# Adaptive-norm modulation in 1024-column pieces summed by transposes, and half of an output projection on both streams at once

## The chip, the cores and the metric

The program runs on one core of one Trainium2 chip. The metric is device time in microseconds (us) of one execution. Before the change it is 2055.41 us (median of 3 runs, 2054.89 to 2059.09).

## What is computed

Two transformer blocks follow one another on 256 tokens of width 1024; the part that matters here is layer 0 of the first. It has two streams, `x` (tile `X` in the kernel, stream 0) and `ctx` (tile `C`, stream 1), each 256 tokens.

```python
for i in range(DEPTH):                       # 2 layers
    mod   = silu(c)     @ w_ada[i] + b_ada[i]   # 6*1024 values, six pieces of 1024
    mod_c = silu(c_ctx) @ w_ada[i] + b_ada[i]
    sh1, sc1, g1, sh2, sc2, g2 = split(mod, 6)
    h = modulate(rms_norm(x), sh1, sc1); hc = the same of ctx with mod_c
    # layer 0: short convolution; layer 1: neighbourhood attention
    b_gate, c_gate, u = split(h @ conv_w_in, 3)
    y = (b_gate * conv3(c_gate * u)) @ conv_w_out
    x = x + g1 * y
    x = x + g2 * swiglu(modulate(rms_norm(x), sh2, sc2), ffn_w_in[i], ffn_w_out[i])
    # and ctx alike with mod_c, in layer 0
```

After it come attention, and a second network of feed-forward blocks and mixers, which the change leaves alone.

## The kernel before

Activations stand transposed, features on partitions and tokens in columns. All weights come through one stream (`WeightStream`): a list of units of 512 KB in the order of use, loaded by SyncE's DMA queue into 5 raw buffers (`raw_bufs`). A unit of a projection is split by ScalarE (`whi`, L106) and VectorE (`wlo`, L107) into a high and a low part, in 4 buffers, and each product is three matmuls (`mm3`, L243 to L245). A unit marked raw is not split. With both streams side by side a matmul has 512 columns, with one stream 256.

The modulation is a matrix times two vectors. The first four pieces of 512 outputs are made by matmuls at the start (`ada_direct`, `ada_fast`); the change touches `ada_slow`, which makes the other 20, (0, 4) to (0, 11) and (1, 0) to (1, 11). For each 128 rows of `w_ada`, VectorE multiplies the rows by one vector's values, one per partition, and adds to an accumulator of 128 x 512 (L476 for the first, L478 for the others), for one vector or for two. The accumulator is split into `ada_hi` and `ada_lo`; TensorE sums it over partitions by matmuls with a selecting matrix `pick` (L489, L490), ScalarE copies the row out, and four small transposes (L441) turn it into columns, to which L444 adds the bias. `ADA_AT` says at which step each piece's four units stand in the stream and are used: after each group of the convolution, after groups of `conv_w_out` for stream 0, and between the groups of the feed-forward.

`conv_block` runs four groups of the convolution's input products (six units a group, 512 columns), then `conv_w_out`: all four groups for stream 0, then all four for stream 1 (256 columns; 16 units). After a stream's groups, its sum of squares goes through matmuls (`rstd_cols`, L361), VectorE makes the inverse square root with ten tiny operations (`newton`, L265 to L269, between L364 and L374), a matmul spreads it over partitions (L376), and `modulate` (L538, L540, then `xh` and `xl`) writes what the feed-forward reads. The first feed-forward group (`ffn`, `first`) uses its four units for stream 0 and then for stream 1, so that stream 0's 96 matmuls run while stream 1 is still being modulated. Earlier, `modulate(0)` and `modulate(1)` inside `conv_block` do the same for the halves of the convolution's input; the second starts with `modA` (L515).

A scheduler decides the order of instructions on each engine when the program is built; each engine then runs its own list in that order.

Of the kernel before, what the change touches and what calls it, by code (L numbers as in the profile page):

```python
# [7 lines left out]
F32 = mybir.dt.float32  # L8
# [7 lines left out]
P = 128  # L16
D = 1024
# [25 lines left out]
def _pack_layout():  # L43
# [15 lines left out]
NPACK = _pack_layout()  # L59
CCOLS = {  # L60
    "ident": (0, 128), "upper": (128, 256), "tri_st": (256, 384),
    "qk_both": (384, 640), "qk_low": (512, 640), "inv_freq": (640, 656), "pick": (656, 660),
}
NCONST = 660

# [100 lines left out]
class Net:  # L166
# [230 lines left out]
    def ada_start(self):  # L397
        nc = self.nc
        sil = self.sil = self.cp.tile([P, 16], F32, name="sil")
        self.pick = self.cp.tile([P, 4], F32R, name="pick")  # L400
        nc.scalar.copy(self.pick, self.k("pick"))
        self.ada_pending = []
        nc.scalar.activation(sil, self.pk[:, 0:16], AF.Silu)
        self.c4 = self.cp.tile([P, KB, 4], F32R, name="c4")
        for v in range(2):
            s = sil[:, 8 * v : 8 * v + 8]
            self.split(self.c4[:, :, 2 * v], self.c4[:, :, 2 * v + 1], s)
# [55 lines left out]

    def ada_slow(self, layer, j, vecs):

        nc = self.nc
        accs = [self.adap.tile([P, 512], F32, name="ada_acc", tag=f"acc{v}") for v in range(vecs)]
        done = 0
        while done < KB:
            w, _, nk, _ = self.ws.take()  # L470
            for kk in range(nk):
                kb = done + kk
                for v in range(vecs):
                    c = self.sil[:, 8 * v + kb : 8 * v + kb + 1]
                    if kb == 0:
                        nc.vector.tensor_scalar(accs[v], w[:, kk, :], c, None, ALU.mult)  # L476
                    else:
                        nc.vector.scalar_tensor_tensor(accs[v], w[:, kk, :], c, accs[v], ALU.mult, ALU.add)  # L478
            done += nk
        parts = []  # L480
        for v in range(vecs):
            hi = self.adap.tile([P, 512], F32R, name="ada_hi", tag="hi")
            lo = self.adap.tile([P, 512], F32R, name="ada_lo", tag="lo")
            self.split(hi, lo, accs[v])
            parts.append((hi, lo))
        yield
        ps = self.aux_bank()
        for v, (hi, lo) in enumerate(parts):
            nc.tensor.matmul(ps[0:2, :], self.pick[:, 2 * v : 2 * v + 2], hi, start=v == 0, stop=False)  # L489
            nc.tensor.matmul(ps[0:2, :], self.pick[:, 2 * v : 2 * v + 2], lo, start=False, stop=v == vecs - 1)  # L490
        row = self.tmp()
        nc.scalar.copy(row[0:2, :], ps[0:2, :])
        yield
        self.ada_columns(layer, j, row)

    def ada_at(self, *at):
        self.ada_pending = [g for g in self.ada_pending if next(g, WAIT) is None]
        for layer, j in ADA_AT.get(at, []):
            g = self.ada_slow(layer, j, ada_vecs(layer, j))
            next(g)  # L500
            self.ada_pending.append(g)

    def ada_flush(self):
        for g in self.ada_pending:
# [40 lines left out]
    def gated_add(self, layer, piece, kb, v, dst, ps):  # L545
        self.nc.vector.scalar_tensor_tensor(dst[:, kb, :], ps, self.mvec(layer, piece, kb, v), dst[:, kb, :], ALU.mult, ALU.add)

    def block_squares(self, src, kb, accs):

        nc = self.nc  # L550
        sq = self.tmp()[:, :T]
        nc.scalar.activation(sq, src[:, kb, :], AF.Square)
        if not accs:
            return [sq]
        if kb == KB - 1:
            return accs + [sq]
        new = self.rp.tile([P, 512], F32, name="acc1", tag="acc")[:, :T]
        nc.vector.tensor_tensor(new, accs[0], sq, ALU.add)
        return [new]


    def ffn(self, xh, xl, sh, sl, parts, evac, between):
# [4 lines left out]
        for part, (b0, b1) in enumerate(parts):  # L567
            for g in range(b0 // 2, b1 // 2):
                gate = [self.main_bank() for _ in range(2)]
                up = [self.main_bank() for _ in range(2)]  # L570
                if first:
                    units = [self.ws.take() for _ in range(4)]
                    for v in range(2):
                        vs = slice(v * T, (v + 1) * T)
                        for i, dst in enumerate((gate, up)):
                            for h in range(2):
                                self.wstat_unit(units[2 * i + h], [d[:, vs] for d in dst], xh[:, :, vs], xl[:, :, vs], k8, 4 * h)
                else:
                    self.wstat(gate, xh, xl, k8)
                    self.wstat(up, xh, xl, k8)  # L580
                first = False
                for c in range(2):
                    blk = 2 * g + c - b0
                    sg = self.tmp()
                    nc.scalar.activation(sg, gate[c], AF.Silu)
                    s = self.tmp()
                    nc.vector.tensor_tensor(s, up[c], sg, ALU.mult)
                    self.split(sh[:, blk, :], sl[:, blk, :], s)
                between("hid", g)
            kall = list(range(b1 - b0))  # L590
            if part == len(parts) - 1:
                for v in range(2):
# [81 lines left out]
ADA_DIRECT = (0, 2)  # L674


ADA_AT = {
    ("conv", 0): [(0, 4)], ("conv", 1): [(0, 5)], ("conv", 2): [(0, 6)], ("conv", 3): [(0, 7)],
    ("conv_out", 0): [(0, 8)], ("conv_out", 2): [(0, 9)],
    ("hid", 0): [(0, 10)], ("hid", 1): [(0, 11)],  # L680
    ("hid", 2): [(1, 0)], ("hid", 3): [(1, 1)], ("hid", 4): [(1, 2)], ("hid", 5): [(1, 3)],
    ("out", 0): [(1, 4)], ("out", 1): [(1, 5)], ("out", 2): [(1, 6)], ("out", 3): [(1, 7)],
    ("hid", 6): [(1, 8)], ("hid", 7): [(1, 9)], ("hid", 8): [(1, 10)], ("hid", 9): [(1, 11)],
}


def ada_specs(w, *at):
    s = []
    for layer, j in ADA_AT.get(at, []):
        s += ada_units(w[layer], j, True)  # L690
    return s


def ada_vecs(layer, j):
    return 2 if layer == 0 or j < 4 else 1


def stream_specs(a):
# [5 lines left out]
    for k0 in (0, 4):  # L704
        for c0 in (1024, 2048):
            s += cols_units(a["conv_w_in"], c0, 256, k8[k0 : k0 + 4])
        if k0 == 0:
            for i in range(2, 4):
                s += ada_units(w[0], ADA_FIRST[i], ADA_FIRST[i] in ADA_DIRECT)
    for g in range(4):  # L710
        for c0 in (1024, 2048, 0) if g > 0 else (0,):
            s += cols_units(a["conv_w_in"], c0 + g * 256, 256, k8)
        s += ada_specs(w, "conv", g)
    for v in range(2):
        for g in range(4):
            s += cols_units(a["conv_w_out"], g * 256, 256, k8)
            if v == 0:
                s += ada_specs(w, "conv_out", g)
    for part, (b0, b1) in enumerate(FFN0_PARTS):
        for g in range(b0 // 2, b1 // 2):  # L720
            s += cols_units(a["ffn_w_in"][0], g * 256, 256, k8)
            s += cols_units(a["ffn_w_in"][0], HID + g * 256, 256, k8)
            s += ada_specs(w, "hid", g)
        for v in range(1 + (part == len(FFN0_PARTS) - 1)):
            for j in range(4):
                s += cols_units(a["ffn_w_out"][0], j * 256, 256, list(range(b0, b1)))
                if part == 0:
                    s += ada_specs(w, "out", j)
# [30 lines left out]
def conv_block(net):  # L759
# [60 lines left out]
        net.wstat_unit(first[i], pcu[i], xh, xl, k8, 0)  # L820
    modulate(1)
    early.close()
    for i in range(2):
        net.wstat_unit(net.ws.take(), pcu[i], xh, xl, k8, 4)
    with tc.tile_pool(name="hid0", bufs=1) as hp, tc.tile_pool(name="ada", bufs=2) as net.adap:
        sh = hp.tile([P, 12, 512], F32R, name="sh")
        sl = hp.tile([P, 12, 512], F32R, name="sl")
        with tc.tile_pool(name="conv", bufs=1) as zp:
# [4 lines left out]
            for g in range(4):  # L833
                if g == 0:
                    pc, pu = pcu
                else:
                    pc = [net.main_bank() for _ in range(2)]
                    net.wstat(pc, xh, xl, k8)
                    pu = [net.main_bank() for _ in range(2)]
                    net.wstat(pu, xh, xl, k8)  # L840
                pb = [net.main_bank() for _ in range(2)]
                net.wstat(pb, xh, xl, k8)
                for c in range(2):
# [13 lines left out]
                net.ada_at("conv", g)  # L857
            for v in range(2):
                accs = []
                for g in range(4):  # L860
                    ps = [net.main_bank()[:, :T] for _ in range(2)]
                    net.wstat(ps, sh[:, :, vsl[v]], sl[:, :, vsl[v]], k8)
                    for c in range(2):
                        net.gated_add(0, 2, 2 * g + c, v, both[v], ps[c])
                        accs = net.block_squares(both[v], 2 * g + c, accs)
                    if v == 0:
                        net.ada_at("conv_out", g)
                if v == 0:
                    net.ada_flush()
                    for half in range(2):  # L870
                        net.mod_scale(0, 1, half)
                net.modulate(0, 1, v, both[v], net.row_stats(accs), k8, xh[:, :, vsl[v]], xl[:, :, vsl[v]])
        state = {}

        def evac(part, j, c, ps, v):
# [1056 lines left out]
```

## Time and profile before

| | |
|---|---|
| median of 3 runs | 2055.41 us |
| the profiled execution | 2058.65 us, its span 2056.7 us |
| TensorE busy (PE) | 2020.6 us, 98% of the span |
| VectorE busy (DVE) | 1522.3 us, 74% |
| ScalarE busy (ACT) | 1060.0 us, 52% |
| mean granted TensorE clock | 0.997 |

The profile's own time is 3.24 us above the median; sums are made against the profile. PE is matmul time, PEld the weight loads beside it. Ends of matmuls are modelled, so a matmul's own duration (0.39 us for 512 columns) is longer than the distance from one start to the next, and it is the distance that adds up.

### The profile page before, as it was taken

The page shows a single profiled execution, that of the slowest core. Times are in us where ns is not written, and L with a number is a line of the kernel's source. Part 1 is how long each engine was busy: PE and PEld are TensorE (multiplying, and loading weights), DVE is VectorE, ACT ScalarE, POOL GpSimd, SP SyncE. Part 2 cuts the span into 40 slices and gives each one's busy share as a digit, 9 for nine tenths or more (in the row PEclk, how much of TensorE's full clock was granted, in tenths as well). Part 3 has the DMA queues.
Part 4 walks back from the last instruction along what each step waited for, and adds up shares of the span by engine and source line. Part 5 has one row for each costly group of instructions (what it writes and reads, how often), then busy time and mean ns, then how long its engine had stood idle before and what let it go on. Part 6 is the DMA issues. An engine that isn't in the chain of part 4 may idle for free. (4 is left out here: it accounts for less than half of the span.)

```text
span 2056.7 us, 32409 instructions
## 1 busy us (share of the span) xinstructions
PE 2020.6 (98%) x12430; PEld 1775.2 (86%) x12430; DVE 1522.3 (74%) x2796; ACT 1060.0 (52%) x1763; POOL 4.1 (0%) x24
## 2 busy tenths in 40 slices
PE   6999999999999999999999999999999999999999
PEld 3888888888899999888888889998888888989888
DVE  6979998766377778766677767787767776887764
ACT  4534533323355566655455546555545555675552
POOL 0000000000000000000000000000000000000000
PEclk9999999999999999999999999999999999999999
DMA  7746566666254324465566564556556656425654
GB/s 251 230 144 195 175 208 199 215 191 200 88 167 146 98 88 138 144 190 180 183 191 188 181 189 132 154 167 192 184 179 191 185 182 193 136 83 168 186 180 133
DMA packets 327435, 350.93 MB, mean 171 GB/s; under 512 B 12593, under 2 KB 301489, under 8 KB 327281
## 3 DMA queue, kind: packets, MB, share of 16 engines
q1 hardware_dynamic: 327280, 348.88, 54.9%
q8 instruction: 97, 1.59, 0.3%
q14 instruction: 58, 0.47, 0.1%
HBM read 347.78 MB, written 1.05 MB: 170 GB/s over the span
## 5 line engine op out<-in xcount | busy, mean ns | idle before, releaser
L106 ACT CAST whi<-wraw 128x512 fp32r<-128x512 f32 (+1 forms) x803 | 615.2, 789 | 714.2 <-issue 252.3
L107 DVE TENSOR_TENSOR wlo<-wraw,whi 128x512 fp32r<-128x512 f32 (+1 forms) x803 | 708.6, 898 | 341.8 <-ACT whi L106 340.5
L306 PE MATMUL pg<-x,whi 128*128 128x512 f32 x1408 | 387.9, 397 | 0.5 <-DVE x L255 0.3
L306 PEld LDWEIGHTS pg<-x,whi 128*128 128x128 f32 x1408 | 241.0, 188 | 33.9 <-DVE x L255 2.8
L306 PE MATMUL po<-s,whi 128*128 128x512 f32 x880 | 243.1, 394 | 0.0
L308 PEld LDWEIGHTS pg<-x,wlo 128*128 128x128 f32 x1408 | 215.1, 188 | 31.8
L308 PE MATMUL pg<-x,wlo 128*128 128x256 f32 x1408 | 223.3, 280 | 0.0
L243 PE MATMUL pm<-xh,whi 128*128 128x512 f32 (+1 forms) x576 | 217.1, 381 | 3.1 <-ACT xh L251 3.1
L244 PE MATMUL pm<-xl,whi 128*128 128x512 f32 (+1 forms) x576 | 218.3, 380 | 0.0
L245 PE MATMUL pm<-xh,wlo 128*128 128x512 f32 (+1 forms) x576 | 218.0, 379 | 0.0
L478 DVE SCALAR_TENSOR_TENSOR ada_acc<-wraw,sil,ada_acc 128x512 f32<-128x512 f32 x224 | 159.3, 747 | 25.1 <-DMA wraw<-in_w_ada 23.9
L306 PEld LDWEIGHTS po<-s,whi 128*128 128x128 f32 x880 | 148.7, 189 | 18.1
L308 PEld LDWEIGHTS po<-s,wlo 128*128 128x128 f32 x880 | 137.5, 188 | 20.6
L308 PE MATMUL po<-s,wlo 128*128 128x256 f32 x880 | 142.6, 280 | 0.0
L243 PEld LDWEIGHTS pm<-xh,whi 128*128 128x128 f32 x576 | 109.3, 191 | 25.5 <-ACT xh L251 3.8
L245 PEld LDWEIGHTS pm<-xh,wlo 128*128 128x128 f32 x576 | 109.2, 190 | 20.5
L244 PEld LDWEIGHTS pm<-xl,whi 128*128 128x128 f32 x576 | 109.4, 190 | 20.3 <-issue 0.2
L245 PE MATMUL pm<-sh,wlo 128*128 128x256 f32 (+1 forms) x384 | 119.2, 311 | 0.4 <-DVE wlo L107 0.4
L243 PE MATMUL pm<-sh,whi 128*128 128x256 f32 (+1 forms) x384 | 119.2, 311 | 0.0
L244 PE MATMUL pm<-sl,whi 128*128 128x256 f32 (+1 forms) x384 | 118.9, 310 | 0.0
L306 PE MATMUL pg<-xh,whi 128*128 128x512 f32 x352 | 97.8, 399 | 1.9 <-DVE xh L252 1.9
L245 PE MATMUL pm<-whi,xl 128*128 128x256 f32 x352 | 99.6, 283 | 0.0
(435 smaller groups left out, 3456.1 us busy)
## 6 DMA issues: line engine op xcount, KB each, us to landing
wraw<-in_ffn_w_in SPq DMA_DIRECT2D x264, 512.0 KB, 3.8
wraw<-in_ffn_w_out SPq DMA_DIRECT2D x128, 512.0 KB, 3.5
wraw<-in_w_ada SPq DMA_DIRECT2D x96, 512.0 KB, 4.5
wraw<-in_a_w_in SPq DMA_DIRECT2D x28, 512.0 KB, 3.7
wraw<-in_conv_w_in SPq DMA_DIRECT2D x24, 512.0 KB, 4.8
wraw<-in_attn_w_qkv SPq DMA_DIRECT2D x24, 512.0 KB, 4.0
wraw<-in_conv_w_out SPq DMA_DIRECT2D x16, 512.0 KB, 4.3
wraw<-in_ffn_w_out SPq DMA_DIRECT2D x28, 256.0 KB, 2.7
```

The source lines that it names most:

```text
L106: self.nc.scalar.copy(hi[:, cs], raw[:, cs])
L107: self.nc.vector.tensor_tensor(lo[:, cs], raw[:, cs], hi[:, cs].bitcast(F32), ALU.subtract)
L243: mm(ps, ah, bh, start=first, stop=False)
L244: mm(ps, ah, bl, start=False, stop=False)
L245: mm(ps, al, bh, start=False, stop=last)
L306: self.nc.tensor.matmul(pss[c], hi[:, kk, cs], x2[:, done + kk], start=done + kk == 0, stop=False)
L308: self.nc.tensor.matmul(pss[c][:, 0, :], lo[:, kk, cs], x2[:, done + kk, 0, :], start=False, stop=done + kk == nblocks - 1)
L478: nc.vector.scalar_tensor_tensor(accs[v], w[:, kk, :], c, accs[v], ALU.mult, ALU.add)
```

## The change

The 20 pieces of 512 outputs become 10 of 1024, (0, 2) to (0, 5) and (1, 0) to (1, 5), eight units of 128 x 1024 each, handed out by `AdaPlan` two or four at a time: after each block of the convolution's weights, between the gate and the up weights of the feed-forward, and after its groups and output groups. None is left between the groups of `conv_w_out`. The sum over partitions is done by transposing the accumulator in 128 x 128 squares (L482 in the new kernel) and reducing on VectorE (L484). The convolution's weights are split 1024 columns at a time. Groups 0 and 1 of `conv_w_out` run on both streams at once (512 columns), groups 2 and 3 for stream 0 and then for stream 1; that takes 12 units in place of 16.

```diff
     def ada_slow(self, layer, j, vecs):
-        accs = [self.adap.tile([P, 512], F32, name="ada_acc", tag=f"acc{v}") for v in range(vecs)]
...
-            hi = self.adap.tile([P, 512], F32R, name="ada_hi", tag="hi")
...
-            nc.tensor.matmul(ps[0:2, :], self.pick[:, 2 * v : 2 * v + 2], hi, start=v == 0, stop=False)
-            nc.tensor.matmul(ps[0:2, :], self.pick[:, 2 * v : 2 * v + 2], lo, start=False, stop=v == vecs - 1)
-        row = self.tmp()
-        nc.scalar.copy(row[0:2, :], ps[0:2, :])
-        yield
-        self.ada_columns(layer, j, row)
+        accs = [self.adap.tile([P, D], F32, name="ada_acc", tag=f"acc{v}") for v in range(vecs)]
+        for kb in range(KB):
+            w = self.ws.take()[0][:, 0, :]
+            for v in range(vecs):
+                c = self.sil[:, 8 * v + kb : 8 * v + kb + 1]
+                if kb == 0:
+                    nc.vector.tensor_scalar(accs[v], w, c, None, ALU.mult)
+                else:
+                    nc.vector.scalar_tensor_tensor(accs[v], w, c, accs[v], ALU.mult, ALU.add)
+            yield
+        col = self.small(16, "ada_sum")
         for v in range(vecs):
+            for h in range(2):
+                pt = self.aux_bank()
+                for b in range(4):
+                    nc.tensor.transpose(pt[:, b * P : (b + 1) * P], accs[v][:, (4 * h + b) * P : (4 * h + b + 1) * P], self.ident)
+                o = 8 * v + 4 * h
+                nc.vector.tensor_reduce(col[:, o : o + 4], pt.rearrange("p (b k) -> p b k", b=4), AX.X, ALU.add)
...
+ADA_UNITS = {("conv", 0, 1): 2, ("conv", 0, 2): 4}
+ADA_UNITS.update({("conv", g, n): 2 for g in range(1, 4) for n in range(3)})
+ADA_UNITS.update({("hid", g, n): 2 for g in range(10) for n in range(2)})
+ADA_UNITS.update({("out", j): 4 for j in range(4)})
...
     early.close()
+    net.ws.width = WeightStream.UNIT
...
+            def conv_out(g, streams):
+                cs = slice(streams[0] * T, (streams[-1] + 1) * T)
+                ps = [net.main_bank()[:, : T * len(streams)] for _ in range(2)]
+                net.wstat(ps, sh[:, :, cs], sl[:, :, cs], k8)
...
+            net.ada_flush()
+            net.ws.width = 512
+            for g in range(2):
+                conv_out(g, (0, 1))
+            for half in range(2):
+                net.mod_scale(0, 1, half)
             for v in range(2):
+                for g in range(2, 4):
+                    conv_out(g, (v,))
+                net.modulate(0, 1, v, both[v], net.row_stats(accs[v]), k8, xh[:, :, vsl[v]], xl[:, :, vsl[v]])
```

What the scheduler made of it shows on two engines. TensorE, in the convolution, where a piece for two vectors is summed; before, a piece of 512 outputs (`pick` is the selecting matrix, `kc` holds the identity):

```order
L441 MATMUL pa<-kc,t 128x2 x4
L489 MATMUL pa<-ada_hi,pick 2x512
L490 MATMUL pa<-ada_lo,pick 2x512
L489 MATMUL pa<-ada_hi,pick 2x512
L490 MATMUL pa<-ada_lo,pick 2x512
L243 MATMUL pm<-xh,whi 128x512
```

and now, a piece of 1024:

```order
L482 MATMUL pa<-kc,ada_acc 128x128 x12
L243 MATMUL pm<-xh,whi 128x512
L244 MATMUL pm<-xl,whi 128x512
L482 MATMUL pa<-kc,ada_acc 128x128 x4
L245 MATMUL pm<-xh,wlo 128x512
```

Sixteen transposes need four PSUM banks and there are three, so the last four stand two matmuls later and need the first bank reduced by VectorE.

VectorE, where `modulate(1)` of the convolution's input starts (`modA` is its scale); before:

```order
L434 TENSOR_TENSOR mod<-ada_col 128x8
L435 TENSOR_TENSOR mod<-mod,pk 128x8
L515 SCALAR_TENSOR_TENSOR modA<-mod,pk 128x8
L107 TENSOR_TENSOR wlo<-wraw,whi 128x512 x2
L252 TENSOR_TENSOR xl<-t,xh 128x512
```

and now:

```order
L433 TENSOR_TENSOR mod<-ada_col 128x8
L473 TENSOR_SCALAR ada_acc<-wraw,sil 128x1024
L434 TENSOR_TENSOR mod<-mod,pk 128x8
L473 TENSOR_SCALAR ada_acc<-wraw,sil 128x1024
L509 SCALAR_TENSOR_TENSOR modA<-mod,pk 128x8
L475 SCALAR_TENSOR_TENSOR ada_acc<-wraw,sil,ada_acc 128x1024 x2
L252 TENSOR_TENSOR xl<-t,xh 128x512 x2
```

Two first products of the new pieces have come ahead of `modA`, and two accumulations ahead of `xl`.

VectorE, inside the inverse square root of stream 1 after `conv_w_out`; before:

```order
L267 SCALAR_TENSOR_TENSOR rc_t<-rc_g 128x2
L478 SCALAR_TENSOR_TENSOR ada_acc<-wraw,sil,ada_acc 128x512
L268 TENSOR_TENSOR rc_t<-rc_t,rc_m 128x2
L478 SCALAR_TENSOR_TENSOR ada_acc<-wraw,sil,ada_acc 128x512
L269 SCALAR_TENSOR_TENSOR rc_g<-rc_t,rc_g 128x2
```

and now:

```order
L267 SCALAR_TENSOR_TENSOR rc_t<-rc_g 128x2
L475 SCALAR_TENSOR_TENSOR ada_acc<-wraw,sil,ada_acc 128x1024
L268 TENSOR_TENSOR rc_t<-rc_t,rc_m 128x2
L475 SCALAR_TENSOR_TENSOR ada_acc<-wraw,sil,ada_acc 128x1024
L269 SCALAR_TENSOR_TENSOR rc_g<-rc_t,rc_g 128x2
```

The pattern holds through the ten steps: between L364 and the spreading of the result (L538 before, L532 now) there stand ten accumulations, 512 columns wide before and 1024 now.

## Rows read from the trace of the kernel before

**Rows 1.** The page: busy time of each engine, share of the span, instructions.

```profile
PE 2020.6 (98%) x12430; PEld 1775.2 (86%) x12430; DVE 1522.3 (74%) x2796; ACT 1060.0 (52%) x1763; POOL 4.1 (0%) x24
```

**Rows 2.** Stages: start:end length, PE, PEld, DVE, ACT, POOL busy (x), clock, DMA, GB/s.

```profile
58.60:180.50 121.90, 121.90 (x543) 99.46 (x542) 107.51 (x172) 47.26 (x85) 0.00 (x0) 1.00 0.59 185
180.50:234.50 54.00, 53.11 (x423) 50.07 (x423) 49.65 (x110) 32.93 (x68) 0.00 (x0) 1.00 0.57 177
234.50:264.50 30.00, 26.99 (x207) 26.33 (x207) 27.38 (x59) 15.14 (x32) 0.00 (x0) 0.94 0.54 167
264.50:562.00 297.50, 297.50 (x1342) 240.55 (x1341) 204.60 (x340) 98.46 (x178) 0.00 (x0) 1.00 0.59 185
```

**Rows 3.** What PE waited for, 58 to 600 us: total, times, longest.

```profile
PE pm L243 <- ACT xh L251: 1.9, 1, 1.9
PE pa L376 <- DVE t L374: 1.1, 1, 1.1
PE pa L489 <- ACT ada_hi L251: 0.5, 1, 0.5
PE pm L245 <- DVE wlo L107: 0.4, 1, 0.4
```

**Rows 4.** Timeline of PE, end of the convolution and first of `conv_w_out`: start, duration.

```profile
171.72 0.39 PE L243 MATMUL pm<-xh,whi 128*128 128x512 f32 x1
...
178.97 0.39 PE L245 MATMUL pm<-xh,wlo 128*128 128x512 f32 x1
...
180.55 0.28 PE L243 MATMUL pm<-sh,whi 128*128 128x256 f32 x1
...
184.50 0.28 PE L243 MATMUL pm<-sh,whi 128*128 128x256 f32 x1
```

**Rows 5.** Transposes of 128 x 128 in attention: timeline of PE around twelve.

```profile
731.65 1.47 PE L1076 MATMUL pa<-kc,t 128*128 128x128 f32 x12
...
733.08 0.28 PE L244 MATMUL pm<-wlo,xh 128*128 128x256 f32 x1
```

**Rows 6.** The same transposes grouped by form: busy, mean ns of one, idle before.

```profile
L1076 PE MATMUL pa<-kc,t 128*128 128x128 f32 x128 | 17.1, 273 | 0.6 <-DVE rc_g L269 0.6
```

**Rows 7.** A stage of attention that holds such transposes, columns as in rows 2.

```profile
790.00:822.00 32.00, 31.38 (x256) 29.32 (x254) 30.53 (x93) 23.06 (x50) 0.00 (x0) 1.00 0.42 133
```

**Rows 8.** DVE groups by form, columns as in rows 6.

```profile
L107 DVE TENSOR_TENSOR wlo<-wraw,whi 128x1024 fp32r<-128x1024 f32 x318 | 388.9, 1223 | 260.4 <-ACT whi L106 260.3
L107 DVE TENSOR_TENSOR wlo<-wraw,whi 128x512 fp32r<-128x512 f32 x484 | 319.5, 686 | 81.4 <-ACT whi L106 80.3
L478 DVE SCALAR_TENSOR_TENSOR ada_acc<-wraw,sil,ada_acc 128x512 f32<-128x512 f32 x224 | 159.3, 747 | 25.1 <-DMA wraw<-in_w_ada 23.9
```

**Rows 9.** Timeline of DVE: stream 1's inverse square root to its first modulation.

```profile
239.63 0.16 DVE L364 TENSOR_SCALAR rc_m<-pa 128x2 f32<-128x2 f32 x1 [0.72 <-PE pa L361]
...
248.91 1.95 DVE L538 TENSOR_TENSOR t<-C,pa 128x256 f32<-128x256 f32 x4 [0.19 <-PE pa L376]
```

**Rows 10.** Timeline of PE there.

```profile
246.85 0.28 PE L245 MATMUL pm<-xh,wlo 128*128 128x256 f32 x1
248.20 0.67 PE L376 MATMUL pa<-t,ones 128*128 128x256 f32 x2 [1.07 <-DVE t L374]
250.80 0.39 PE L243 MATMUL pm<-xh,whi 128*128 128x256 f32 x1 [1.93 <-ACT xh L251]
```

**Rows 11.** The stage after that gap, columns as in rows 2.

```profile
252.50:255.00 2.50, 2.50 (x13) 2.50 (x13) 2.50 (x5) 2.50 (x7) 0.00 (x0) 0.50 0.02 7
```

**Rows 12.** Timeline of DVE: `modA` of the convolution's input, and a wait for weights.

```profile
56.03 0.17 DVE L515 SCALAR_TENSOR_TENSOR modA<-mod,pk 128x8 f32<-128x8 f32 x1
...
106.70 0.89 DVE L476 TENSOR_SCALAR ada_acc<-wraw,sil 128x512 f32<-128x512 f32 x2 [3.97 <-DMA wraw<-in_w_ada]
```

**Rows 13.** Timeline of PE at the first matmul on that modulation's output.

```profile
58.37 0.39 PE L245 MATMUL pm<-xh,wlo 128*128 128x512 f32 x1
58.59 0.62 PE L243 MATMUL pm<-xh,whi 128*128 128x512 f32 x2
```

More of the change, by code (lines that the diff above doesn't have):

```diff
@@ L61 @@
     "ident": (0, 128), "upper": (128, 256), "tri_st": (256, 384),
-    "qk_both": (384, 640), "qk_low": (512, 640), "inv_freq": (640, 656), "pick": (656, 660),
+    "qk_both": (384, 640), "qk_low": (512, 640), "inv_freq": (640, 656),
 }
@@ L399, in ada_start @@
         sil = self.sil = self.cp.tile([P, 16], F32, name="sil")
-        self.pick = self.cp.tile([P, 4], F32R, name="pick")
-        nc.scalar.copy(self.pick, self.k("pick"))
+        self.ada_plan = AdaPlan()
         self.ada_pending = []
@@ L466, in ada_slow @@
         nc = self.nc
-        accs = [self.adap.tile([P, 512], F32, name="ada_acc", tag=f"acc{v}") for v in range(vecs)]
[L468 to L479, printed above, removed]
@@ L480, in ada_slow @@
-        parts = []
-        for v in range(vecs):
-            hi = self.adap.tile([P, 512], F32R, name="ada_hi", tag="hi")
-            lo = self.adap.tile([P, 512], F32R, name="ada_lo", tag="lo")
-            self.split(hi, lo, accs[v])
-            parts.append((hi, lo))
-        yield
-        ps = self.aux_bank()
-        for v, (hi, lo) in enumerate(parts):
-            nc.tensor.matmul(ps[0:2, :], self.pick[:, 2 * v : 2 * v + 2], hi, start=v == 0, stop=False)
-            nc.tensor.matmul(ps[0:2, :], self.pick[:, 2 * v : 2 * v + 2], lo, start=False, stop=v == vecs - 1)
@@ L491, in ada_slow @@
-        row = self.tmp()
-        nc.scalar.copy(row[0:2, :], ps[0:2, :])
-        yield
-        self.ada_columns(layer, j, row)
-    def ada_at(self, *at):
-        self.ada_pending = [g for g in self.ada_pending if next(g, WAIT) is None]
[L498 to L501, printed above, removed]
+        accs = [self.adap.tile([P, D], F32, name="ada_acc", tag=f"acc{v}") for v in range(vecs)]
@@ new lines, in ada_slow, with ada_at @@
+        bias = self.p(f"b_ada{layer}")[:, 8 * j : 8 * j + 8, None].to_broadcast([P, 8, vecs])
+        nc.vector.tensor_tensor(self.mod[:, layer, 8 * j : 8 * j + 8, 0:vecs], col[:, : 8 * vecs].rearrange("p (v b) -> p b v", b=8), bias, ALU.add)
+    def ada_at(self, *step):
+        self.ada_pending = [g for g in self.ada_pending if next(g, WAIT) is None]
+        for layer, j, kb in self.ada_plan.at(step):
+            if kb == 0:
+                self.ada_piece = self.ada_slow(layer, j, ada_vecs(layer, j))
+            next(self.ada_piece)
+            if kb == KB - 1:
+                self.ada_pending.append(self.ada_piece)
@@ L546, in gated_add, with block_squares @@
         self.nc.vector.scalar_tensor_tensor(dst[:, kb, :], ps, self.mvec(layer, piece, kb, v), dst[:, kb, :], ALU.mult, ALU.add)
-    def block_squares(self, src, kb, accs):
+    def block_squares(self, src, kb, accs, pool=None):
         nc = self.nc
@@ L556, in block_squares @@
             return accs + [sq]
-        new = self.rp.tile([P, 512], F32, name="acc1", tag="acc")[:, :T]
+        new = (pool or self.rp).tile([P, 512], F32, name="acc1", tag="acc", bufs=2)[:, :T]
         nc.vector.tensor_tensor(new, accs[0], sq, ALU.add)
@@ L579, in ffn @@
                     self.wstat(gate, xh, xl, k8)
+                    between("hid", g, 0)
                     self.wstat(up, xh, xl, k8)
-                first = False
                 for c in range(2):
@@ L588, in ffn @@
                     self.split(sh[:, blk, :], sl[:, blk, :], s)
-                between("hid", g)
+                if first:
+                    between("hid", g, 0)
+                first = False
+                between("hid", g, 1)
             kall = list(range(b1 - b0))
@@ L674, with __init__, at, specs @@
 ADA_DIRECT = (0, 2)
[L677 to L691, printed above, removed]
+ADA_UNITS = {("conv", 0, 1): 2, ("conv", 0, 2): 4}
+ADA_UNITS.update({("conv", g, n): 2 for g in range(1, 4) for n in range(3)})
+ADA_UNITS.update({("hid", g, n): 2 for g in range(10) for n in range(2)})
+ADA_UNITS.update({("out", j): 4 for j in range(4)})
+class AdaPlan:
+    def __init__(self):
+        pieces = [(0, j) for j in range(2, 6)] + [(1, j) for j in range(6)]
+        self.units = iter([(layer, j, kb) for layer, j in pieces for kb in range(KB)])
+    def at(self, step):
+        return [next(self.units) for _ in range(ADA_UNITS.get(step, 0))]
+    def specs(self, w, *step):
+        return [wspec(w[layer], kb, 1, j * D, D, True) for layer, j, kb in self.at(step)]
 def ada_vecs(layer, j):
-    return 2 if layer == 0 or j < 4 else 1
+    return 2 if layer == 0 or j < 2 else 1
 def stream_specs(a):
@@ L709, in stream_specs @@
                 s += ada_units(w[0], ADA_FIRST[i], ADA_FIRST[i] in ADA_DIRECT)
+    plan = AdaPlan()
     for g in range(4):
[L711 to L718, printed above, removed]
+        for n, c0 in enumerate((1024, 2048, 0)):
+            if g > 0 or n == 2:
+                s += cols_units(a["conv_w_in"], c0 + g * 256, 256, k8)
+            s += plan.specs(w, "conv", g, n)
+    for g in (0, 1, 2, 3, 2, 3):
+        s += cols_units(a["conv_w_out"], g * 256, 256, k8)
     for part, (b0, b1) in enumerate(FFN0_PARTS):
         for g in range(b0 // 2, b1 // 2):
-            s += cols_units(a["ffn_w_in"][0], g * 256, 256, k8)
-            s += cols_units(a["ffn_w_in"][0], HID + g * 256, 256, k8)
-            s += ada_specs(w, "hid", g)
+            gate = cols_units(a["ffn_w_in"][0], g * 256, 256, k8)
+            up = cols_units(a["ffn_w_in"][0], HID + g * 256, 256, k8)
+            if g == 0:
+                s += gate + up + plan.specs(w, "hid", g, 0)
+            else:
+                s += gate + plan.specs(w, "hid", g, 0) + up
+            s += plan.specs(w, "hid", g, 1)
         for v in range(1 + (part == len(FFN0_PARTS) - 1)):
@@ L727, in stream_specs @@
                 if part == 0:
-                    s += ada_specs(w, "out", j)
+                    s += plan.specs(w, "out", j)
     for q in range(4):
@@ L838, in conv_block @@
                     net.wstat(pc, xh, xl, k8)
+                    net.ada_at("conv", g, 0)
                     pu = [net.main_bank() for _ in range(2)]
                     net.wstat(pu, xh, xl, k8)
+                net.ada_at("conv", g, 1)
                 pb = [net.main_bank() for _ in range(2)]
@@ L856, in conv_block @@
                     net.split(sh[:, kb, :], sl[:, kb, :], y)
-                net.ada_at("conv", g)
-            for v in range(2):
[L859 to L872, printed above, removed]
+                net.ada_at("conv", g, 2)
+            accs = [[], []]
+            def conv_out(g, streams):
+                cs = slice(streams[0] * T, (streams[-1] + 1) * T)
+                ps = [net.main_bank()[:, : T * len(streams)] for _ in range(2)]
+                net.wstat(ps, sh[:, :, cs], sl[:, :, cs], k8)
+                for c in range(2):
+                    for i, v in enumerate(streams):
+                        net.gated_add(0, 2, 2 * g + c, v, both[v], ps[c][:, vsl[i]])
+                        accs[v] = net.block_squares(both[v], 2 * g + c, accs[v], (None, zp)[v])
+            net.ada_flush()
[4 more added lines that the diff above has]
+                net.mod_scale(0, 1, half)
+            for v in range(2):
+                for g in range(2, 4):
+                    conv_out(g, (v,))
+                net.modulate(0, 1, v, both[v], net.row_stats(accs[v]), k8, xh[:, :, vsl[v]], xl[:, :, vsl[v]])
         state = {}
```

## The prediction, made blind

> **What bounds the kernel now.** I read the busy line of the page first: TensorE is busy for 2020.6 of 2056.7 us [rows 1], so a change is worth what it takes off TensorE's own list, plus or minus the time in which TensorE stands still. The table by stage says where that is. In the convolution (58.6 to 180.5) and in most of the first feed-forward (264.5 to 562) PE is busy without a hole; it loses 0.9 us in `conv_w_out` (180.5 to 234.5) and 3.0 us in the stage behind it, where the granted clock is also 0.94 [rows 2]. The list of PE's waits names them: 0.4 for a split of weights, 0.5 for `ada_hi`, and then 1.1 for the spread of stream 1's inverse square root and 1.9 for its first `xh` [rows 3]. VectorE is the second engine to look at: 107.5 of 121.9 us in the convolution and 49.7 of 54.0 in `conv_w_out` [rows 2], so work added to it there can become a wait of PE. DMA engines are 0.57 to 0.59 busy there [rows 2] and load the same w_ada bytes as before; I leave them out but for one place below.
>
> **What PE's list loses and gains.** With 512 columns matmuls start 0.2266 us apart (32 steps from 171.72 to 178.97), with 256 columns 0.1197 (33 steps from 180.55 to 184.50) [rows 4].
>
> *Old sums, out.* A piece for two vectors stands between the matmul at 178.97 and that at 180.55: 1.58 less one step is 1.35 us. One vector has two of the four `pick` matmuls: 1.35 less two steps is 0.90. Twelve pieces are for two vectors, eight for one: 12 x 1.35 + 8 x 0.90 = 23.4 us off.
>
> *Transposes, in.* The trace has the same form, f32 128 x 128 against the identity. Twelve of them begin at 731.65 and the second matmul after them at 733.08 [rows 5]; less one step of 0.12 that is 1.31 us for twelve, 0.11 each. Six pieces for two vectors have 16, four for one have 8: 128 x 0.11 = 14.1 us on. One row speaks for a higher price: each alone lasts 273 ns [rows 6], which would be 34.9 us for 128, 20.8 more; but busy time of all 128 in attention is only 17.1 us [rows 6], so they overlap, and I take 0.11. The Trainium skill ("TensorE: Matmul & The Clock Gate", Part 4: PE-mode transpose) gives about 275 ns for one in a kernel and says that the clock gate does not count a transpose as busy the same way. By the trace the duration agrees (273); taken as the price, the page's figure would make the sum some 21 us dearer. As for the clock, the stage of attention from 790 to 822 holds such transposes and has a granted clock of 1.00 [rows 7].
>
> *`conv_w_out`.* Groups 0 and 1 were 192 matmuls of 256 columns and become 96 of 512: 23.0 against 21.8 us, 1.2 off. That is little because a wide step costs nearly two narrow ones. The four units less to split only unload ScalarE and VectorE.
>
> *The small waits* for `ada_hi` and the split (0.5 and 0.4) go, since no piece stands in `conv_w_out` any more: 0.9 off.
>
> So far 23.4 - 14.1 + 1.2 + 0.9 = 11.4 us off.
>
> **What comes back as waiting.** VectorE's list decides it.
>
> *Stream 1's modulation.* Between L364 and the spread result VectorE took from 239.63 to 248.91 [rows 9], with ten accumulations of 512 columns among the ten tiny steps. They are now 1024 wide, with nothing to wait for. No 1024-wide accumulation is in the trace. The split grows from 686 to 1223 ns with the same widening, 0.54 us [rows 8]; twice the accumulation's own 747 ns would be 0.75 more. I take the first, since each has a fixed part that does not double: 10 x 0.54 = 5.4 us (bounds 7.5, and 4.8 if the statistics begin 0.6 earlier, which their place on PE's list would allow). The cover does not grow: stream 0's 96 matmuls, which ended at 246.85 with the gap already open [rows 10]. So PE's gap from 246.85 to 250.80, 3.95 us, becomes about 9.3. All 5.4 count.
>
> *The clock behind the gap.* From 252.5 to 255 the clock was 0.50, the lower level, and PE ran 13 matmuls [rows 11] where full speed gives 21. A longer gap may stretch that: 0 to 1.5 us, taken 0.5.
>
> *`modulate(1)`.* The first matmul on its output starts at 58.59, one step behind the one before it [rows 13]: no slack. Two 1024-wide first products now stand ahead of `modA`, which ran at 56.03. Two 512-wide ones take 0.89 [rows 12], so 0.9 to 1.8 us; taken 1.1, for the same fixed part, all of it waited for.
>
> *Stream 0's modulation* used to have eight groups of stream 1 (four of `conv_w_out`, 192 matmuls) as cover and has 96 now. Its inverse square root has only two splits among the steps in place of ten fillers, so it fits but for the spreading matmul, which PE's list places 44 matmuls after the stream's last: 0 to 1.5, taken 0.8.
>
> *A load.* Among stream 1's first modulations VectorE accumulates the piece's seventh unit, whose raw buffer comes free only with the sixth. The list has 3.2 us between; a load behind a freed buffer made VectorE wait 3.97 us [rows 12]. 0 to 2, taken 0.7, since `xl` of blocks 2 and 3 is queued behind it.
>
> *The last four transposes* of each two-vector piece need a bank that VectorE must first reduce. PE issues twelve (1.3 us) and two to four matmuls (0.5 to 0.9), then waits. The first four results are there after some 0.7 us and a reduction of 512 elements takes some 0.69 as the split does [rows 8], so 0.4 to 0.8 us are spare if VectorE is idle then. It will not always be: counted off the lists, its work from the first piece to the first `conv_w_out` result is 118 us now (42 accumulations at 1.2, 22 wide splits at 1.14, 12 reductions at 0.6, the rest as before) against 110 (70 accumulations at 0.67, 45 half splits at 0.6), in a stage of 125. One accumulation in the way costs up to 1.2. Six places: 0 to 7, taken 2.0.
>
> Together 5.4 + 0.5 + 1.1 + 0.8 + 0.7 + 2.0 = 10.5 us on. **Sum:** 10.5 - 11.4 = -0.9. Against the profiled execution (2058.65, span 2056.7) that is 2057.8; that execution lies 3.2 above the median of 2055.41, so for a median 2054.5. Behind the first feed-forward PE's list is the same, save its line numbers.
>
> **Rivals.** 0.2% is 4.1 us, about what a measurement tells from no change.
>
> *Faster.* The waits that I sized by lists do not arise: VectorE has time at every reduction, the buffers come early, stream 0 is in time, the clock does not fall longer. Left is the chain of stream 1 at its lower bound: -11.4 + 4.8 = -6.6, 2048.8 us. For it: PE has not one hole in the convolution though VectorE is 88% busy, and pieces now come evenly, two units between two. Against: `modulate(1)` has no slack. 0.23.
>
> *Slower: VectorE sets the pace at the transposes.* Each of the six places late by a whole 1024-wide accumulation and part of a split, 1.5 us: 9.0 in place of 2.0, so +6.1, 2061.5 us. It decides from 1.2 us a place on (7.0 in all, +4.1). For it: 118 of 125 us of work in the convolution and a fixed list; against: the feed-forward's 204.6 of 297.5 us [rows 2]. 0.24.
>
> *The transposes do not overlap* here and cost their 273 ns: +20.8 - 0.9 = +19.9, 2075.3 us. Against it stand the rows of twelve [rows 5, 6], whose data were f32 as here. The skill's 275 ns and its remark on the clock would give this or worse; the trace so far bears out neither. 0.03.
>
> *The forecast*: 0.50, from -4 to +4 around the old time.
>
> **Chances and range.** Faster by over 0.2%: 0.23; within it: 0.50; slower: 0.27 (0.24 and 0.03). The range 2047.5 to 2062.5 takes in the centres of the first two rivals and leaves out the third and the tails.
>
> **What the profile will show.** The transposes 0.11 us apart at clock 1.00; groups 0 and 1 of `conv_w_out` in 21.8 us; PE starting `modulate(1)`'s output about 1 us late; no hole inside `conv_w_out` but one below 1.5 us at L376; a gap of 9 us before stream 1's first feed-forward matmul, with ten 1024-wide accumulations of about 1.2 us on VectorE beside it; small waits of PE for a reduction at some of the six places. I am wrong if the gap stays at 4 us (then it is faster by some 6), or if PE's waits in the convolution add up to over 7 (then slower).

## The result, and the profile after

The changed kernel takes 2063.86 us (median of 7, 2062.23 to 2065.78), the kernel before, run beside it, 2058.83 (median of 7): ratio 1.0028, 95% interval 1.0016 to 1.0039. So it is slower by 5 us, where 0.9 less was forecast. The forecast of 2054.5 stood on the first three runs of before (2055.41); all seven have a median 3.4 higher, so 3.4 of the 9.4 us between forecast and measurement belong to the base and not to the change. The profiled execution has a span of 2061.9 us against 2056.7, so the two traces differ by what the runs differ by.

First the page: busy time of each engine, share of the span, instructions.

```profile
PE 2011.6 (98%) x12318; PEld 1770.6 (86%) x12318; DVE 1497.0 (73%) x2628; ACT 1026.3 (50%) x1680; POOL 4.1 (0%) x24
```

PE is busy for 9.0 us less than before [rows 1], and the span is 5.2 longer: PE's list did shrink, and PE now stands still for 14 us more. Where, the list of PE's waits between 50 and 600 us says (total, times, longest):

```profile
PE pa L482 <- DVE ada_sum L484: 7.7, 4, 2.5
PE pa L376 <- DVE t L374: 6.2, 1, 6.2
PE pm L243 <- ACT xh L251: 4.0, 2, 2.1
```

Of [rows 3] the two waits in `conv_w_out` are gone, L376 has grown from 1.1 to 6.2, `xh` has a second wait of 2.1, and at the top stands a new one: transposes (L482) that wait for VectorE's reductions (L484). By stage, cut at the same events as [rows 2]: the idle before `modulate(1)`'s output, the convolution, `conv_w_out`, the first group of the feed-forward, its rest, and two spells of it (start:end length, PE, PEld, DVE, ACT, POOL busy (x), clock, DMA, GB/s):

```profile
58.60:60.50 1.90, 0.00 (x0) 0.00 (x0) 1.90 (x2) 1.90 (x5) 0.00 (x0) 1.00 1.02 340
60.50:188.70 128.20, 125.15 (x573) 103.67 (x573) 110.22 (x122) 42.83 (x58) 0.00 (x0) 1.00 0.62 193
188.70:235.90 47.20, 47.14 (x304) 42.73 (x303) 33.26 (x77) 20.82 (x43) 0.00 (x0) 1.00 0.37 112
235.90:271.00 35.10, 26.92 (x204) 25.93 (x204) 31.84 (x54) 16.17 (x34) 0.00 (x0) 0.85 0.55 165
271.00:569.80 298.80, 294.08 (x1331) 243.53 (x1331) 186.72 (x258) 81.51 (x145) 0.00 (x0) 0.99 0.57 180
258.00:261.00 3.00, 2.96 (x14) 2.96 (x15) 2.09 (x5) 3.00 (x7) 0.00 (x0) 0.50 0.29 112
309.00:312.00 3.00, 3.00 (x9) 2.36 (x8) 3.00 (x6) 0.00 (x0) 0.00 (x0) 0.51 0.51 169
```

The convolution and the feed-forward had no hole before and now have holes of 3.0 and 4.7 us: the 7.7. `conv_w_out` has none any more. The gap before stream 1's first matmul is worth 8.2 us of idle. The last row is new too: behind one of the waits for reductions, of 2.24 us, the clock is at its lower level for some 3 us, which it was nowhere in this stage before.

One two-vector piece, PE's timeline first, then VectorE's (start, duration, ..., idle before and its releaser):

```profile
104.27 1.47 PE L482 MATMUL pa<-kc,ada_acc 128*128 128x128 f32 x12
105.50 0.48 PE L243 MATMUL pm<-xh,whi 128*128 128x512 f32 x1
105.81 0.40 PE L244 MATMUL pm<-xl,whi 128*128 128x512 f32 x1
108.15 0.66 PE L482 MATMUL pa<-kc,ada_acc 128*128 128x128 f32 x4 [1.95 <-DVE ada_sum L484]
```

```profile
103.77 1.27 DVE L475 SCALAR_TENSOR_TENSOR ada_acc<-wraw,sil,ada_acc 128x1024 f32<-128x1024 f32 x1
104.96 0.68 DVE L855 TENSOR_TENSOR z<-pm,t 128x512 f32<-128x512 f32 x1
105.56 1.27 DVE L475 SCALAR_TENSOR_TENSOR ada_acc<-wraw,sil,ada_acc 128x1024 f32<-128x1024 f32 x1
106.76 0.74 DVE L858 SCALAR_TENSOR_TENSOR t<-z,pk,t 128x512 f32<-128x512 f32 x1
107.42 2.47 DVE L484 TENSOR_REDUCE ada_sum<-pa 128x4 f32<-128x512 f32 x4
```

Twelve transposes take 1.23 us and fill the three auxiliary banks. VectorE reaches its first reduction only at 107.42: two accumulations and two steps of the convolution stand ahead of it in its list. The last four transposes need that bank, and PE, two matmuls later, stands until the first reduction is done.

The two longest waits, in the feed-forward, come about otherwise. VectorE and PE at the first of them:

```profile
305.26 2.48 DVE L475 SCALAR_TENSOR_TENSOR ada_acc<-wraw,sil,ada_acc 128x1024 f32<-128x1024 f32 x2 [2.74 <-DMA wraw<-in_w_ada]
307.66 2.47 DVE L484 TENSOR_REDUCE ada_sum<-pa 128x4 f32<-128x512 f32 x4
```

```profile
308.39 0.66 PE L482 MATMUL pa<-kc,ada_acc 128*128 128x128 f32 x4 [2.24 <-DVE ada_sum L484]
```

The first twelve transposes had begun at 303.74. VectorE was not full but idle: it waited 2.74 us for the load of a unit of the next piece, because two accumulations of that piece stand ahead of the reductions in its list. At the other place it waited 2.76 us for such a load, with three accumulations ahead.

Stream 1's chain on VectorE and PE beside it:

```profile
241.54 0.16 DVE L364 TENSOR_SCALAR rc_m<-pa 128x2 f32<-128x2 f32 x1 [0.55 <-PE pa L361]
...
250.57 1.27 DVE L475 SCALAR_TENSOR_TENSOR ada_acc<-wraw,sil,ada_acc 128x1024 f32<-128x1024 f32 x1
251.77 0.15 DVE L268 TENSOR_TENSOR rc_t<-rc_t,rc_m 128x2 f32<-128x2 f32 x1
251.84 1.27 DVE L475 SCALAR_TENSOR_TENSOR ada_acc<-wraw,sil,ada_acc 128x1024 f32<-128x1024 f32 x1
...
254.30 0.47 DVE L374 TENSOR_SCALAR t<-kc,rcol 128x128 f32<-128x128 f32 x2
254.69 1.27 DVE L475 SCALAR_TENSOR_TENSOR ada_acc<-wraw,sil,ada_acc 128x1024 f32<-128x1024 f32 x1
256.15 1.95 DVE L532 TENSOR_TENSOR t<-C,pa 128x256 f32<-128x256 f32 x4 [0.18 <-PE pa L376]
```

```profile
248.40 0.28 PE L245 MATMUL pm<-xh,wlo 128*128 128x256 f32 x1
254.92 1.19 PE L376 MATMUL pa<-t,ones 128*128 128x256 f32 x2 [6.24 <-DVE t L374]
258.05 1.22 PE L243 MATMUL pm<-xh,whi 128*128 128x256 f32 x4 [1.93 <-ACT xh L251]
```

L364 to L532 takes 14.6 us (9.3 in [rows 9]): each tiny step of 0.15 us waits for the 1024-wide accumulation ahead of it, 1.27 us. The two matmuls that spread the result (L376) take 1.19 us in place of 0.67, since the granted clock is at 0.50 there. PE's gap is 9.65 us, against 3.95 in [rows 10].

### The profile page after: what moved, and what is told of

Read it like the earlier page. It is cut to its first block, busy times and chain, and to the rows that moved or that the text cites. A ratio compares the mean times of both kernels' runs of the same rounds, so it can differ in the third digit from the quotient of the medians.

```text
span 2061.9 us, 31882 instructions
## 1 busy us (share of the span) xinstructions
PE 2011.6 (98%) x12318; PEld 1770.6 (86%) x12318; DVE 1497.0 (73%) x2628; ACT 1026.3 (50%) x1680; POOL 4.1 (0%) x24
## 5 line engine op out<-in xcount | busy, mean ns | idle before, releaser
L106 ACT CAST whi<-wraw 128x512 fp32r<-128x512 f32 (+2 forms) x773 | 607.5, 808 | 735.4 <-issue 218.9
L107 DVE TENSOR_TENSOR wlo<-wraw,whi 128x512 fp32r<-128x512 f32 (+2 forms) x773 | 701.1, 921 | 365.5 <-ACT whi L106 362.3
L475 DVE SCALAR_TENSOR_TENSOR ada_acc<-wraw,sil,ada_acc 128x1024 f32<-128x1024 f32 x112 | 141.1, 1279 | 53.7 <-DMA wraw<-in_w_ada 53.6
L243 PE MATMUL pm<-sh,whi 128*128 128x256 f32 (+1 forms) x352 | 113.9, 323 | 0.0
L245 PE MATMUL pm<-sh,wlo 128*128 128x256 f32 (+1 forms) x352 | 113.7, 323 | 0.0
L244 PE MATMUL pm<-sl,whi 128*128 128x256 f32 (+1 forms) x352 | 113.2, 322 | 0.0
```

Source lines behind the costliest of these rows:

```text
L106: self.nc.scalar.copy(hi[:, cs], raw[:, cs])
L107: self.nc.vector.tensor_tensor(lo[:, cs], raw[:, cs], hi[:, cs].bitcast(F32), ALU.subtract)
L243: mm(ps, ah, bh, start=first, stop=False)
L244: mm(ps, ah, bl, start=False, stop=False)
L245: mm(ps, al, bh, start=False, stop=last)
L475: nc.vector.scalar_tensor_tensor(accs[v], w, c, accs[v], ALU.mult, ALU.add)
```

## Experiments

Theory A: the loss is three waits of PE that add up, for reductions (7.7), for stream 1's chain (5.3 more than before) and for `modulate(1)` (2.1). Rivals: B, VectorE is full, so a wait removed comes back elsewhere; C, the new work on PE or the clock is dear; D, the shared half of `conv_w_out` took cover away. Each kernel starts from the changed one unless said otherwise; medians of before in the two groups of runs (e1 to e4, then e5 to e8) are 2058.02 and 2057.63. The changed kernel was not run again with them, so a difference from its 2063.86 carries the 0.8 or 1.2 us by which these lie below 2058.83.

**Four auxiliary banks (e4).**

```diff
-        self.banks(5, 3)
+        self.banks(4, 4)
```

> Four auxiliary PSUM banks and four main ones in place of three and five, so that the sixteen transposes of a two-vector piece need no bank that VectorE must first reduce. Theory A (the bank is what PE waits for): the four waits for reductions (7.7 us in all) go; if four main banks are enough, 2056 us; if PE now waits for main banks, these waits are named after the convolution's or the gated adds' lines and eat up what was gained, 2058 to 2064. Rival B (not the bank but VectorE's lateness as such): 2063 or more, with waits of PE on VectorE elsewhere in the convolution.

Measured: 2055.57 us, ratio 0.9984 (0.9975 to 0.9993), 8.3 less than the changed kernel. All sixteen transposes now stand in one row, and the list of waits has no L482 and no new line in the convolution:

```profile
106.61 1.91 PE L482 MATMUL pa<-kc,ada_acc 128*128 128x128 f32 x16
108.28 0.48 PE L243 MATMUL pm<-xh,whi 128*128 128x512 f32 x1
```

It is the bank. VectorE's reductions are as late as before (its first at 109.6, 1.3 us after PE has gone on), but nobody waits for them. B falls here.

**Stream 1's chain without accumulations (e2).**

```diff
+ADA_UNITS.update({("hid", 0, 0): 0, ("hid", 0, 1): 0, ("hid", 1, 0): 0})
+ADA_UNITS.update({("hid", g, 0): 3 for g in range(2, 8)})
```

> The six units of modulation weights of the first two steps of the feed-forward are taken in six later steps, so that no 1024-wide accumulation stands between stream 1's L364 and L532. Theory A (5.3 us of the loss, and the 4 us gap of before, are that chain): L364 to L532 falls from 14.6 us to about 5, PE's gap of 9.4 us before stream 1's first feed-forward matmul nearly closes, and the spell at clock 0.50 behind it goes (1.4 us): 2063.9 - 9.4 - 1.4 = 2053 us; 2056 if only half of the gap closes. Rival B (accumulations must be done somewhere and VectorE is full): the gap closes, but PE's waits on VectorE in the later groups grow by as much, 2062 to 2066 us.

Measured: 2048.84 us, ratio 0.9957 (0.9944 to 0.9969), 15.0 less than the changed kernel and 9.2 less than before. VectorE's chain:

```profile
242.29 0.16 DVE L364 TENSOR_SCALAR rc_m<-pa 128x2 f32<-128x2 f32 x1 [0.46 <-PE pa L361]
...
247.27 1.95 DVE L532 TENSOR_TENSOR t<-C,pa 128x256 f32<-128x256 f32 x4 [0.91 <-PE pa L376]
```

5.0 us in place of 14.6, and the list of PE's waits from 50 to 600 us keeps only a remnant of L376:

```profile
PE pa L482 <- DVE ada_sum L484: 3.2, 2, 1.7
PE pm L243 <- ACT xh L251: 2.2, 1, 2.2
PE pa L376 <- DVE t L374: 0.2, 1, 0.2
```

It came out 4 us better than A expected, because the pieces in the feed-forward now end at other places, where VectorE is in time: the two waits for reductions there (4.7) are gone, those in the convolution (3.0, now 3.2) are not. This was not expected. The opposite of B happened. (`xh` here is `modulate(1)`'s wait, left as it was.)

**Nothing ahead of `modulate(1)` (e3).**

```diff
+ADA_UNITS.update({("conv", 0, 1): 0, ("conv", 0, 2): 0})
+ADA_UNITS.update({("conv", g, n): 3 for g in range(1, 4) for n in range(2)})
```

> The first six units of modulation weights are moved behind modulate(1), so that modA is not queued behind first products; from then on three units stand where two stood, in six steps. Theory A (2.1 us of the loss are that delay): the wait of 2.06 us at the first matmul on modulate(1)'s output falls below 0.5, 2062 us. Rival B (VectorE is full in the convolution): the wait goes, but the waits for reductions at the transposes (3.0 us in the convolution) grow by 2 us or more: 2063 to 2067 us.

Measured: 2058.51 us, ratio 1.0003 (0.9994 to 1.0011), 5.4 less than the changed kernel. The wait of 2.06 is gone, and the waits for reductions are 4.7 us in place of 7.7, since with other counts per step the pieces end elsewhere. 2.1 and 3.0 make 5.1. A's part holds; what B expected, that these waits grow in the convolution, is refuted: there they fell from 3.0 to 0.8.

**Each half of the change alone (e5, e7).** e5 is the changed kernel with `conv_w_out` stream by stream; e7 is the kernel before with the shared half (its pieces and sums as before). The edit of e5, which e7 makes the other way round:

```diff
-            for g in range(2):
-                conv_out(g, (0, 1))
...
             for v in range(2):
-                for g in range(2, 4):
-                    conv_out(g, (v,))
+                accs = []
+                for g in range(4):
+                    ps = [net.main_bank()[:, :T] for _ in range(2)]
+                    net.wstat(ps, sh[:, :, vsl[v]], sl[:, :, vsl[v]], k8)
...
```

> The pieces alone: as after, but conv_w_out goes stream by stream as before. Theory A (the loss comes from the pieces: waits for reductions, stream 1's chain, modulate(1)): 2065 us, that is after plus the 1.2 us which the wide matmuls save; waits of PE as in after. Rival D (the loss comes from the shared half of conv_w_out, which halves the cover of stream 0's modulation and of stream 1's): the gap before stream 1's first feed-forward matmul falls below 6 us and the time is 2059 us or less.

> Half of conv_w_out on both streams alone, put into the kernel before, with its 512-column pieces and their sums as before. Theory A: 1.2 us less than before, near 2057 us, with the gap before stream 1's first feed-forward matmul at 4 us as before. Rival D (cover): stream 0's modulation has 96 matmuls in place of 192 beside it and comes late, or stream 1's gap grows, by 2 us or more: 2059 to 2063 us.

Measured: the pieces alone 2067.54 us, ratio 1.0049 (1.0036 to 1.0061); the shared half alone 2056.53, ratio 0.9991 (0.9982 to 1.0000), 1.1 less than before (0 to 3.7 by the interval). D falls: all of the loss is in the pieces. e7 waits as before does (L376 1.2, `xh` 1.9). In e5 the waits for reductions are worse:

```profile
PE pa L482 <- DVE ada_sum L484: 10.1, 4, 3.8
PE pm L243 <- ACT xh L251: 4.2, 2, 2.2
PE pa L376 <- DVE t L374: 3.4, 1, 3.4
```

while L376's is 2.9 shorter, since this list has L364 at 244.55, 9.9 us ahead of stream 0's last feed-forward matmul (254.41), where the changed kernel has 6.9 (241.54 and 248.40). So D has a grain of truth, 3 us of this wait, that the time of e5 does not show. e5 is 2.5 us above what A expected. Its profiled execution (2071.47) is the slowest of its five, with spells at the lower clock near 62, 158 and 363 us that the changed kernel's trace lacks; how much of the 2.5 is the clock and how much the longer waits for reductions stays open.

**Column sums by matmuls in place of transposes and reductions (e1).**

```diff
-            for h in range(2):
...
-                nc.vector.tensor_reduce(col[:, o : o + 4], pt.rearrange("p (b k) -> p b k", b=4), AX.X, ALU.add)
+            for b in range(8):
+                nc.tensor.matmul(pt[:, 8 * v + b : 8 * v + b + 1], accs[v][:, b * P : (b + 1) * P], self.ones[:, 0:1], start=True, stop=True)
```

> Sums over partitions by one-column matmuls (accumulator block as weights, a column of ones as moving data) in place of transposes and VectorE reductions; one bank holds all results. Theory A (7.7 us of the loss are PE waiting for VectorE's reductions before the last four transposes of a two-vector piece): these waits vanish, PE's price of the sums stays near 0.11 us each, so 2063.9 - 7.7 = 2056 us, and no new wait of 1 us or more in the convolution. Rival B (VectorE is full there, so the lateness only moves to another wait): at most 2 us come back, 2062 or more, with new waits of PE on VectorE in the convolution. Rival C (the new PE work itself is dear): 2064 or above.

Measured: 2085.76 us, ratio 1.0131 (1.0118 to 1.0144), 21.9 more than the changed kernel. The waits for reductions are gone, as A has it, but my price was wrong. PE's timeline at the first run of sums and at the sixth, and the stage behind the first (columns as above):

```profile
104.55 4.53 PE L480 MATMUL pa<-ones,ada_acc 128*128 128x1 f32 x32
108.94 0.77 PE L243 MATMUL pm<-xh,whi 128*128 128x512 f32 x1
...
419.67 3.63 PE L480 MATMUL pa<-ones,ada_acc 128*128 128x1 f32 x32
423.15 0.49 PE L243 MATMUL pm<-sh,whi 128*128 128x512 f32 x1
```

```profile
109.00:113.50 4.50, 4.50 (x12) 3.53 (x12) 4.38 (x6) 0.00 (x0) 0.00 (x0) 0.50 0.55 165
```

Sixteen sums are 32 matmuls, each with its own load of weights. At clock 1.00 they take 3.49 us (the run at 419.67), 0.22 a sum; in the run at 104.55 the clock falls on the way, and they take 4.39. I had read 0.11 from pairs at L361, without seeing that a pair is one f32 product. At clock 1.00 the sums are 10.9 us dearer than the transposes for six pieces (3.49 against 1.67 in e4) and 3.6 for four (1.70 against 0.79); with the 7.7 saved, 6.9 more. The remaining 15 is mostly the clock, which is at its lower level for 3 to 7 us from within or just behind each of the six long runs, near 107, 158, 196, 319, 366 and 424 us, some 30 us in all. C is true of this kernel, not of the changed one.

**Every transpose twice (e8)**, on e4, so that no wait hides the price.

```diff
-                for b in range(4):
+                for b in (0, 1, 2, 3) * 2:
```

> Every transpose is issued twice, on the kernel with four auxiliary banks, so that no wait hides or shows the price. Theory A (0.104 us each, overlapped): 13.4 us more than the kernel with four banks, near 2069 us, a run of 32 transposes taking 3.4 us at clock 1.00. Rival C (273 ns each, or a fall of the clock behind a run of transposes): 2090 us, or 2 us and more beyond 2069 with the clock at 0.50 behind the runs.

Measured: 2066.4 us in one run, its span 10.7 over that of e4's profile. PE's timeline, and the stage behind it:

```profile
104.13 3.65 PE L482 MATMUL pa<-kc,ada_acc 128*128 128x128 f32 x32
107.54 0.48 PE L243 MATMUL pm<-xh,whi 128*128 128x512 f32 x1
```

```profile
107.50:113.00 5.50, 5.50 (x27) 4.59 (x26) 5.50 (x9) 0.00 (x0) 0.00 (x0) 1.00 0.30 97
```

32 in 3.41 us, 0.107 each; 128 more are 13.6. The span shows 3 less, because this trace is 2.5 us ahead of e4's before any transpose (104.13 against 106.61), and e4's has a spell at the lower clock near 856 us that this one lacks. Between the first run of transposes and the start of the last (561.35 here, 550.18 in e4) the 120 more take 13.65 us, 0.114 each. 35 more (273 ns each) is out, and so is a fall of the clock: it is 1.00 behind the longest run of transposes here. C falls.

**The three remedies together (e6)**: the edits of e4, e2 and e3.

> Three remedies on the changed kernel at once: four auxiliary banks, no modulation units in the first two steps of the feed-forward up to (1, 0), none ahead of modulate(1). Theory A (three waits of PE that add up, none of which moves elsewhere): 2063.9 less 8.3 (the banks, as run alone), 10.5 (the chain, 15.0 as run alone without the 4.5 us of waits for reductions that went with it) and 2.1 (modulate(1), without the 3.0 us of such waits): 2043 us. Rival B (VectorE is full, so part of the work comes back as waits): 2047 us or more, no better than the chain's remedy alone.

Measured: 2042.55 us, ratio 0.9924 (0.9911 to 0.9936): 15.1 less than before, 21.3 less than the changed kernel, and the best of all runs. PE's waits from 50 to 600 us, and the first group of the feed-forward:

```profile
PE pm L243 <- ACT xh L251: 1.0, 1, 1.0
PE pa L376 <- DVE t L374: 0.2, 1, 0.2
```

```profile
236.00:262.00 26.00, 26.00 (x190) 24.72 (x189) 22.52 (x44) 14.05 (x27) 0.00 (x0) 1.00 0.55 173
```

Of the 17.9 us that the changed kernel waited there, 1.2 are left. The gains add up as A said, so what was wrong with the change is its waits and nothing else of this size.

## Why the prediction was wrong

**The step that failed** is the one on the last four transposes of a piece, sized at 2.0 us (0 to 7). It measured 7.7, at four of six places (1.0, 1.9, 2.2, 2.5), and 1.6 more by the clock behind one of them (eight matmuls from 309.14 to 312.53 take 3.39 us, 1.81 at 0.2266 each). The mechanism was in the text, as a term and as the second rival (from 7.0 on); its size, and so the order of forecast and rival, was not. I had compared 118 us of VectorE's work with a stage of 125 and concluded that it was mostly in time. In the convolution's stage VectorE was busy for 110.2 of 128.2 us, less than I had counted, and PE waited all the same. Such a sum says nothing of a moment: the wait hangs on which instructions stand directly ahead of the first reduction, which could have been read off the list, place by place, and on whether their inputs are there. The two worst places lie in the feed-forward, where VectorE was busy for 204.6 of 297.5 us [rows 2] and which I counted as evidence against. It was no fuller after the change (186.7 of 298.8): there it stood idle for 2.7 us for a load of the next piece, at the head of its list, while the reductions that PE needed stood behind. e4 shows that PE waits for the bank, e2, e3 and e5 that the size goes with the place (3.2, 4.7, 10.1).

The other terms, in the order of the text:
- *Old sums, out*: 23.4 holds. Counted over the trace of before, from the matmul ahead of a group to the one behind it, less one step, four sums take 0.93, two take 0.47 and a group of small transposes (L441) 0.42: 12 x 0.93 + 8 x 0.47 + 20 x 0.42 = 23.3.
- *Transposes, in*: 14.1 holds. Sixteen take 1.67 us in e4, 0.104 each, and change-over matmuls bring a piece to 1.8. The Trainium skill ("TensorE: Matmul & The Clock Gate", Part 4: PE-mode transpose) gives about 275 ns for one in a kernel and says that the gate does not count a transpose as PE-busy in the same way. The trace agrees on one transpose's duration (272), not on that as a price in a row; and no fall of the clock followed even 32 of them.
- *`conv_w_out`*: 1.2 and the small waits 0.9 hold: no wait of [rows 3] there is left, and e7, which has neither of the small waits either, measures 1.1 (0 to 3.7) for both together.
- *Stream 1's chain*: 5.4 forecast, 5.3 measured, in part by luck. The right rows had been read: the ten accumulations were known by name. But the tenth stands behind L374, beside the spreading matmuls, so nine count: L364 to L374 grew from 7.95 us (239.63 to 247.58) to 12.76, by 4.8. The other 0.5 is the spreading matmuls at the lower clock. PE's gap is 9.65 for about 9.3; it grew by 5.7, since L364 also stands 0.4 us nearer to the end of stream 0's matmuls.
- *The clock behind the gap*: 0.5 forecast. Behind the gap it is 0.50 from 258 to 261.2 and was from 252 to 255 before: nothing. It cost its 0.5 ahead, in L376.
- *`modulate(1)`*: 1.1 forecast, 2.06 measured. `modA` runs at 58.23, 2.2 later than in [rows 12], 1.1 of that by a spell at the lower clock ahead of it, so the chain is late by what I said; but PE's list also has the first matmul on its output six matmuls (1.36 us) further up than before: the cover moved, which I had not looked for.
- *Stream 0's modulation* 0.8 and *the load* 0.7: no wait of PE is named there. Both nothing.

Sum of what was measured, to the end of the first feed-forward, with the gap's growth of 5.7: -23.3 + 14.4 - 1.2 - 0.9 + 5.7 + 2.1 + 7.7 + 1.6 = +6.1. The traces put the same matmul 8.1 later there (569.76 against 561.67), 1.1 of it from ahead of all that changed (56.53 against 55.42), mostly the longer spell near 40 us; of the other 7.0, 0.9 is not accounted for. Behind, the traces draw together by 2.9, of which 1.8 is a spell in the trace of before (0.91 over 840 to 860) that the other lacks. Such spells come and go between the traces, and why stays open. The one near 40 us lasts some 7 us in seven of the eight traces with the new pieces, and some 3 us in e8 and in both with the old ones (before, e7), so a part of the change in it is not ruled out.

## What to carry to other kernels

Where an engine with a fixed list must free a buffer for the bottleneck engine, its share of busy time does not tell the wait: look which instructions stand ahead of the freeing one and whether one of them waits for a load, and give the bottleneck a buffer more before giving the other engine wider instructions. Tiny steps interleaved with fillers take the fillers' time (nine fillers, each 0.53 us longer, made the steps up to L374 4.8 us longer), so keep long fillers out of a chain whose end the bottleneck waits for. And measure a price on whole groups, from the start of the matmul ahead to the start of the one behind: a pair of matmuls that is one f32 product is easily counted wrong.

## What the runs showed of the hardware

At a granted clock of 1.00, a one-column f32 product with a 128 x 128 block as weights costs 0.22 us in a row (16 in 3.49, e1) and two instructions, a transpose of the same block 0.104 (16 in 1.67, e4) and one. Within or just behind each of the six runs of 16 such products the granted clock fell to 0.50; behind 16 transposes in a row (e4) and behind 32 (3.41 us, e8) it stayed at 1.00. And waits of PE of about 2 us are not alike: behind those at 308 us (2.24) the clock fell to 0.5 for 3 us, behind those at 108 (1.95) and 358 (2.48) it did not.
